# Input projections as seven products of mixed blocks, with values transposed, the residual in DRAM and fp32 scores

## The chip, the core and the metric

The kernel runs on one core of a Trainium2 chip. TensorE (PE in the profile, PEld its weight load) does the matmuls, VectorE (DVE), ScalarE (ACT) and GpSimd (POOL) the elementwise work, and SyncE's queue (SPq) issues every DMA. The metric is the device time of one execution in microseconds (us), lower is better.

## What is computed

One inference step of a two-layer decoder over 1024 prompt tokens and 8 sample tokens, model width 1024, all in fp32. Layer 0 is sliding-window attention (window 128, 32 heads of 64, 4 key/value heads), layer 1 is retention (4 heads, 256 wide in q and k, 512 in v). Each layer has one wide input projection, a gated mixer and an output projection:

```python
h = _rmsnorm(x, norm_g[i])
q, k, v, g = split(h @ w_in)                 # 1024 -> 4608 (layer 0) or 6144 (layer 1) features
logits = q k^T / 8 + bias(rel);  w = softmax with a learned sink;  o = w v      # layer 0
o = (q k^T * decay) v + q R * cross;  R = gamma R + k_dec^T v;  o = norm(o)     # layer 1
x = x + (silu(g) * o) @ w_out
y = _rmsnorm(x, final_norm_g)
```

## The kernel before

Activations stand with features on the partitions. The tokens go in two halves: half A is tokens 0 to 511 with the 8 samples (520 columns), half B is tokens 512 to 1023. An fp32 operand of a large matmul is split into a rounded high part and the rest (`hi` and `lo`, type fp32r), and a product is three matmuls: hi\*hi, lo\*hi, hi\*lo (lines 359 to 361).

**The weight stream.** `Stream` holds a list of jobs and of weight tiles (128x512). `wload` (line 171) loads a tile by DMA into `wraw` (3 buffers), ACT casts it to `whi` (line 175), and DVE and POOL in turn make `wlo = wraw - whi` (line 179). `AHEAD = 2` keeps two further tiles on the way, and `whi` and `wlo` have four buffers each. `proj_job` makes 128 features of the input projection from two tiles, in chunks of 260 columns (half A) or 512 (half B); `tok_job` makes values with tokens on the partitions; `out_job` and `out1_job` do the output projections, one tile for 128 features, and add to the residual `xa`, which stays in SBUF for one half at a time.

**The order of the work.** PE's order is written by hand: `spread` lays the jobs of the stream between the steps of the mixers. Layer 0 goes through 64 blocks of 4 heads and 128 queries (`att_scores`, `att_turn`, `att_values`), four key/value heads u for half A, then four for half B. Layer 1 goes through n = 0 to 7 (four heads for A, four for B). Each n has three stages: **a**, the output projection of n-1 (8 tiles); **b**, the gates of n+1 (two feature pairs); **c**, q, k and v of n+1 (four feature pairs of work). The other engines take their instructions in an order that the tile framework's scheduler writes at build time, and each works through its queue in order. `norm` makes the 8 normalised `hh`/`hl` tiles of a half, `rot_jobs` applies the rotary angles to q and k of layer 1, and `norm_stats` makes the row factors.

Of the kernel before, what the change touches and what calls it, by code (L numbers as in the profile page):

```python
# [19 lines left out]
P = 128  # L20
D = 1024
KT = 8
# [26 lines left out]

AHEAD = 2  # L50
SLACK = 600.0
# [7 lines left out]

class Stream:  # L60
# [4 lines left out]
    def __init__(self, load, ahead):  # L65
        self.load, self.ahead = load, ahead
        self.jobs = []
        self.todo, self.ready = [], []

    def push(self, srcs, fn, ns):  # L70
        self.todo += srcs
        self.jobs.append([fn, None, ns])
# [5 lines left out]
    def fetch(self, n):  # L78
        while self.todo and len(self.ready) < n:
            self.ready.append(self.load(self.todo.pop(0)))  # L80
# [30 lines left out]
def hybrid_step(ctx: ExitStack, tc: tile.TileContext, I: dict, O: dict):  # L111
# [4 lines left out]
    xp = ctx.enter_context(tc.tile_pool(name="xp", bufs=1))  # L116
# [16 lines left out]

    def chunks(T):
        return [(0, 512)] if T == HALF else [(0, 260), (260, 520)]


    xT = [None] * KT
    xdram = [[dp.tile([P, HALF], F32, name=f"xdram{hf}_{kt}") for kt in range(KT)] for hf in range(2)]
    xsmp = cp.tile([P, KT, NB], F32, name="xsmp")  # L140

    def load_x(srcs, T):
        for kt in range(KT):
            xa = xp.tile([P, HALF + NB], F32, name="xa", tag=f"x{kt}")
            sp.dma_start(xa[:, :T], srcs[kt])
            xT[kt] = xa

    def store_x(hf):
        for kt in range(KT):
            sp.dma_start(xdram[hf][kt], xT[kt][:, 0:HALF])  # L150
# [19 lines left out]

    def wload(src):
        raw = wp.tile([P, 512], F32, name="wraw", tag="wr", bufs=3)
        last[0] = sp.dma_start(raw, src)
        hi = wp.tile([P, 512], F32R, name="whi", tag="wh", bufs=4)
        act.copy(hi, raw)  # L175
        lo = wp.tile([P, 512], F32R, name="wlo", tag="wl", bufs=4)
        wctr[0] += 1
        eng = pool if wctr[0] % 2 else vec
        eng.tensor_tensor(out=lo, in0=raw, in1=r32(hi), op=ALU.subtract)  # L179
        return hi, lo  # L180

    stream = Stream(wload, 0)


    H = [None]

    def stats_rows(s, T):
# [5 lines left out]
        for b in range(4):  # L193
            pe.matmul(ps[:, b : b + 1], s[:, b * P : (b + 1) * P], ones[:, 0:1], start=True, stop=True)
        if T > HALF:
            pe.matmul(ps[:NB, 4:5], s[:, SMP], ones[:, 0:1], start=True, stop=True)
# [5 lines left out]
    def stats_spread(rs, T, tag):  # L202

        dg = ap_.tile([P, T], F32, name="dg", tag="sq", bufs=3)
# [7 lines left out]
        rb_ = ap_.tile([P, T], F32, name="rbc", tag=tag, bufs=1)  # L212
# [7 lines left out]
    def norm_stats(T, tag, out, stored=None):  # L220

        s = None
        for kt in range(KT):
            b = ap_.tile([P, T], F32, name="sqb", tag="sq", bufs=3)
            if stored is None:
                x = xT[kt][:, :T]
            else:
                x = b
                sp.dma_start(b, stored[kt])
            act.activation(b, x, AF.Square)  # L230
# [5 lines left out]
        rs = stats_rows(s, T)  # L236
        yield
        out.append(stats_spread(rs, T, tag))
        yield

    def norm(layer, T, rb_, src):

        hh, hl = [], []
        H[0] = (hh, hl, None, T)
        rb_ = [rb_.pop()]
        for kt in range(KT):
            f = ap_.tile([P, T], F32, name="hf", tag="sq", bufs=3)
            vec.scalar_tensor_tensor(out=f, in0=src(kt, f), scalar=gcol[:, layer, kt : kt + 1], in1=rb_[0], op0=ALU.mult, op1=ALU.mult)
            a = hp.tile([P, T], F32R, name=f"hh{kt}")
            b = hp.tile([P, T], F32R, name=f"hl{kt}")  # L250
            act.copy(a, f)
            (pool if kt % 2 else vec).tensor_tensor(out=b, in0=f, in1=r32(a), op=ALU.subtract)
            hh.append(a)
            hl.append(b)
            if kt % 2 and kt < KT - 1:
                yield
        if T > HALF:
            hs = cp.tile([P, KT, 40], F32R, name="hs", tag="hs")
            pool.memset(r32(hs), 0.0)
            for kt in range(KT):  # L260
                vec.tensor_copy(hs[:, kt, 0:NB], r32(hh[kt][:, SMP]))
                vec.tensor_copy(hs[:, kt, 32 : 32 + NB], r32(hl[kt][:, SMP]))
            H[0] = (hh, hl, hs, T)
        yield

    def stored_x(tiles, smp=False):
        def get(kt, f):
            sp.dma_start(f[:, 0:HALF], tiles[kt])
            if smp:
                vec.tensor_copy(f[:, SMP], xsmp[:, kt, :])  # L270
            return f

        return get

    def final_norm(hf, T):

        out = []
        yield from norm_stats(T, "rbc", out)
        for kt in range(KT):
            f = ap_.tile([P, T], F32, name="hf", tag="sq", bufs=3)  # L280
            vec.scalar_tensor_tensor(out=f, in0=xT[kt][:, :T], scalar=gcol[:, 2, kt : kt + 1], in1=out[0], op0=ALU.mult, op1=ALU.mult)
            sp.dma_start(O["yT"][kt, :, hf * HALF : hf * HALF + T], f)
        yield

    def final_part(c0, c1):

        w = c1 - c0
        xs = [xT[kt][:, c0:c1] for kt in range(KT)]
# [20 lines left out]
        if smp:  # L309
            fo = [ap_.tile([P, 2, w], F32, name="fo", tag="y", bufs=6) for _ in range(4)]  # L310
# [37 lines left out]
    def proj_job(src, evac):  # L348

        def run():  # L350
            hh, hl, _, T = H[0]
            out = [(gtile()[:, : c1 - c0], c0, c1) for c0, c1 in chunks(T)]
            for z in range(2):
                hi, lo = stream.tile()
                for ps, c0, c1 in out:
                    for i in range(4):
                        k = 4 * z + i
                        a, b = hi[:, i * P : (i + 1) * P], lo[:, i * P : (i + 1) * P]
                        pe.matmul(ps, a, hh[k][:, c0:c1], start=(k == 0), stop=False)  # L359
                        pe.matmul(ps, a, hl[k][:, c0:c1], start=False, stop=False)  # L360
                        pe.matmul(ps, b, hh[k][:, c0:c1], start=False, stop=(k == KT - 1))  # L361
                    if z:
                        evac(ps, c0, c1)
                    yield 12 * mm_ns(c1 - c0)

        stream.push([src[0], src[1]], run, 5200.0)

    def tok_job(srcs, width, smp, evac):


        per = 512 // width

        def run():
            hh, hl, hs, T = H[0]
            pss = [gtile()[:, :width] for _ in range(4)]
            if smp:
                pss.append(sps.tile([P, 1024], F32, name="vsp", tag="S")[:40, :width])
            for z in range(KT // per):
                hi, lo = stream.tile()
                for b, ps in enumerate(pss):  # L380
                    for i in range(per):
                        k = z * per + i
                        wh, wl = hi[:, i * width : (i + 1) * width], lo[:, i * width : (i + 1) * width]
                        if b < 4:
                            cs = slice(b * P, (b + 1) * P)
                            pe.matmul(ps, hh[k][:, cs], wh, start=(k == 0), stop=False)  # L386
                            pe.matmul(ps, hh[k][:, cs], wl, start=False, stop=False)  # L387
                            pe.matmul(ps, hl[k][:, cs], wh, start=False, stop=(k == KT - 1))  # L388
                        else:
                            pe.matmul(ps, hs[:, k, :], wh, start=(k == 0), stop=False)  # L390
                            pe.matmul(ps, hs[:, k, :], wl, start=False, stop=(k == KT - 1))
                    if k == KT - 1:
                        evac(b, ps)
                yield 14 * per * mm_ns(width)

        stream.push(list(srcs), run, KT * 14 * mm_ns(width))

    def sample_rows(ps, width):
        t = ap_.tile([NB, width], F32, name="srow", tag="s", bufs=SB)
        act.copy(t, ps[32 : 32 + NB, :])  # L400
        vec.tensor_tensor(out=t, in0=t, in1=ps[0:NB, :], op=ALU.add)
        return t

    def out_job(T, src, ys, fts):

        for ft in fts:
            def run(ft=ft):
                hi, lo = stream.tile()
                for c0, c1 in chunks(T):
                    ps = gtile()[:, : c1 - c0]  # L410
                    for k in range(4):
                        yh, yl = ys[k // 2]
# [4 lines left out]
                    x = xT[ft][:, c0:c1]  # L417
# [3 lines left out]
            stream.push([src[ft]], run, 2600.0)  # L421
# [3 lines left out]
    def new_y(tag="y", bufs=6):  # L425
# [931 lines left out]
```

## Time and profile before

| what | value |
|---|---|
| median of 3 runs | 1739.86 us (the fastest 1739.23) |
| profiled execution | 1736.38 us, span 1734.6 us |
| PE | 1697.7 us busy, 98% of the span |
| DVE, ACT, POOL | 1045.5 (60%), 841.1 (48%), 713.2 (41%) |
| granted TensorE clock | 0.994 |
| DMA | 211.31 MB, 122 GB/s over the span |

The span is the profiled execution from the first to the last instruction; the median stands 3.5 us above that execution's own time. A busy PE counts a matmul from its start to its modelled end, and matmuls overlap, so the spacing of starts is the cost of one, not its mean duration.

### The profile page before, as it was taken

How to read it: one execution, taken by the hardware profiler on the slowest of the kernel's cores; microseconds unless marked ns; L12 is line 12 of the kernel's file. 1: busy time of each engine (PE TensorE's matmuls, PEld its weight loads, DVE VectorE, ACT ScalarE, POOL GpSimd, SP SyncE). 2: the span in 40 equal slices, each digit the busy share in tenths (PEclk: the TensorE clock that was granted, in tenths of full speed). 3: DMA queues.
4: the chain of work that ended last, by engine and by line, in shares of the span. 5: the costliest groups of instructions: out<-in, count | busy, mean ns of one | idle time of the engine just before them, and what ended most of it. 6: DMA issues, size and time to landing. Idle time of an engine off the chain costs nothing.

```text
span 1734.6 us, 29003 instructions
## 1 busy us (share of the span) xinstructions
PE 1697.7 (98%) x10550; PEld 1450.0 (84%) x10550; DVE 1045.5 (60%) x2142; ACT 841.1 (48%) x1960; POOL 713.2 (41%) x670
## 2 busy tenths in 40 slices
PE   9999999999999999999999999999999999999997
PEld 8989999988887777779788797897777889888887
DVE  6777676784576565773475545566555655445366
ACT  5566465555556464654344444344343433433344
POOL 3244344353344343444334235344353353433534
PEclk9999999999999999999999999999999999999998
DMA  5523333333253323223476445466463262322323
GB/s 153 142 62 91 123 105 104 89 108 91 85 172 90 85 75 92 80 86 106 120 244 192 143 152 188 128 195 206 129 217 111 85 194 73 98 86 81 102 69 121
DMA packets 124174, 211.31 MB, mean 122 GB/s; under 512 B 17128, under 2 KB 28000, under 8 KB 124032
## 3 DMA queue, kind: packets, MB, share of 16 engines
q1 hardware_dynamic: 124032, 209.47, 39.5%
q8 instruction: 83, 1.36, 0.3%
q14 instruction: 59, 0.48, 0.1%
HBM read 177.57 MB, written 33.91 MB: 122 GB/s over the span
## 4 chain that ended last, share of the span: by engine, by line
PE 81%; DVE 5%; DMA 3%; ACT 2%; POOL 2%; issue 1%; SPq 0%; POOLq 0%; ACTq 0%; DVEq 0%
PE gemm L359 12%; PE gemm L360 12%; PE gemm L361 12%; PE gemm L386 4%; PE gemm L387 3%; PE gemm L388 3%; PE o L663 3%; PE gemm L1063 3%; PE gemm L1062 3%; PE gemm L1064 3%; PE gemm L414 3%; PE gemm L416 3%; PE gemm L415 3%; PE S L624 3%; PE pt L641 1%
## 5 line engine op out<-in xcount | busy, mean ns | idle before, releaser
L179 POOL TENSOR_TENSOR wlo<-wraw,whi 128x512 fp32r<-128x512 f32 x236 | 311.7, 1321 | 555.6 <-ACT whi L175 524.0
L359 PE MATMUL gemm<-hh,whi 128*128 128x260 f32 (+1 forms) x1584 | 520.9, 329 | 0.0
L361 PE MATMUL gemm<-hh,wlo 128*128 128x260 f32 (+1 forms) x1584 | 506.2, 320 | 0.4 <-POOL wlo L179 0.4
L360 PE MATMUL gemm<-hl,whi 128*128 128x260 f32 (+1 forms) x1584 | 506.2, 320 | 0.0
L175 ACT CAST whi<-wraw 128x512 fp32r<-128x512 f32 x472 | 290.5, 617 | 442.9 <-PE gemm L360 136.5
L359 PEld LDWEIGHTS gemm<-hh,whi 128*128 128x128 f32 x1584 | 298.2, 188 | 45.0 <-issue 15.3
L361 PEld LDWEIGHTS gemm<-hh,wlo 128*128 128x128 f32 x1584 | 298.0, 188 | 23.3 <-POOL wlo L179 0.6
L360 PEld LDWEIGHTS gemm<-hl,whi 128*128 128x128 f32 x1584 | 298.5, 188 | 20.2 <-issue 0.5
L179 DVE TENSOR_TENSOR wlo<-wraw,whi 128x512 fp32r<-128x512 f32 x236 | 190.1, 806 | 161.6 <-ACT whi L175 159.5
L431 POOL TENSOR_TENSOR yl<-yf,yh 128x256 fp32r<-128x256 f32 x128 | 107.3, 847 | 96.7 <-ACT yh L430 96.3
L414 PE MATMUL gemm<-yh,whi 128*128 128x260 f32 (+1 forms) x384 | 126.9, 330 | 4.4 <-DVE xa L418 4.4
L386 PE MATMUL gemm<-whi,hh 128*128 128x512 f32 (+1 forms) x320 | 123.1, 385 | 2.9 <-DVE ra L748 2.8
L598 ACT ACTIVATE L<-L,nm 128x128 f32<-128x128 f32 x256 | 99.8, 391 | 52.2 <-DVE nm L593 51.8
L1062 PE MATMUL gemm<-yh,whi 128*128 128x260 f32 (+3 forms) x384 | 124.7, 325 | 0.0
L416 PE MATMUL gemm<-yh,wlo 128*128 128x260 f32 (+1 forms) x384 | 123.2, 321 | 0.0
L415 PE MATMUL gemm<-yl,whi 128*128 128x260 f32 (+1 forms) x384 | 123.0, 320 | 0.0
L1063 PE MATMUL gemm<-yl,whi 128*128 128x260 f32 (+3 forms) x384 | 122.8, 320 | 0.0
L1064 PE MATMUL gemm<-yh,wlo 128*128 128x260 f32 (+3 forms) x384 | 122.8, 320 | 0.0
L388 PE MATMUL gemm<-whi,hl 128*128 128x512 f32 (+1 forms) x320 | 120.0, 375 | 2.0 <-DVE hl L1099 1.8
L387 PE MATMUL gemm<-wlo,hh 128*128 128x512 f32 (+1 forms) x320 | 120.4, 376 | 0.0
L602 POOL TENSOR_TENSOR L<-L,rsum 128x512 f32<-128x512 f32 x64 | 76.4, 1193 | 79.3 <-DVE rsum L601 45.4
L414 PEld LDWEIGHTS gemm<-yh,whi 128*128 128x128 f32 x384 | 72.6, 189 | 15.2 <-ACT whi L175 4.8
(246 smaller groups left out, 3141.8 us busy)
## 6 DMA issues: line engine op xcount, KB each, us to landing
wraw<-in_w_in SPq DMA_DIRECT2D x264, 256.0 KB
wraw<-in_w_out SPq DMA_DIRECT2D x136, 256.0 KB
wraw<-in_w_v SPq DMA_DIRECT2D x72, 256.0 KB
Rsm<-in_state SPq DMA_DIRECT2D x64, 256.0 KB
out_ret_state_sample<-Rsm SPq DMA_DIRECT2D x64, 256.0 KB
vrow<-vdram SPq DMA_DIRECT2D x32, 256.0 KB
bias<-bdram SPq DMA_DIRECT2D x16, 256.0 KB
xdram<-xa SPq DMA_DIRECT2D x16, 256.0 KB
```

The costliest lines, as they stand in the source:

```text
L175: act.copy(hi, raw)
L179: eng.tensor_tensor(out=lo, in0=raw, in1=r32(hi), op=ALU.subtract)
L359: pe.matmul(ps, a, hh[k][:, c0:c1], start=(k == 0), stop=False)
L360: pe.matmul(ps, a, hl[k][:, c0:c1], start=False, stop=False)
L361: pe.matmul(ps, b, hh[k][:, c0:c1], start=False, stop=(k == KT - 1))
L386: pe.matmul(ps, hh[k][:, cs], wh, start=(k == 0), stop=False)
L414: pe.matmul(ps, a, yh[:, k % 2, c0:c1], start=(k == 0), stop=False)
L415: pe.matmul(ps, a, yl[:, k % 2, c0:c1], start=False, stop=False)
L416: pe.matmul(ps, b, yh[:, k % 2, c0:c1], start=False, stop=(k == 3))
L1062: pe.matmul(ps, a, yh[:, k % 2, c0:c1], start=(k == 0), stop=False)
L1063: pe.matmul(ps, a, yl[:, k % 2, c0:c1], start=False, stop=False)
L1064: pe.matmul(ps, b, yh[:, k % 2, c0:c1], start=False, stop=(k == 3))
```

## The change

**Projections.** A pair of 128-feature blocks, over the two quarters of a half's tokens (256 columns and 256 or 264) and the two halves of the 1024 input features, is a 2x2 product of blocks. It is now made by seven products of mixed blocks instead of eight (`unit_job`). The seven activation mixtures of a half are made once by `mixtures`, each split into hi and lo; the seven weight mixtures are made for each pair by `mixed`, from four loaded tiles, each split into hi and lo. A product is 12 matmuls and takes one split tile. Raw weight tiles have 7 buffers, and loads go 3 further tiles ahead (`DEEP`).

```diff
+    def mixed(wa, wb):
...
+        def third():
+            minus(d["a"], d["b"], d["a"], vec)
+            d["t"] = wtile()
+            return wsplit(minus(d["t"], d["d"], d["a"], vec), vec)
+        return [
+            Weights(get(a=wa[0]), lambda: wsplit(d["a"], pool)),
+            Weights(get(c=wa[1]), lambda: wsplit(d["c"], pool)),
+            Weights(get(b=wb[0], d=wb[1]), third),
+            Weights(None, lambda: wsplit(d["a"], pool)),
+            Weights(None, lambda: wsplit(minus(d["b"], d["d"], d["b"], pool), vec)),
+            Weights(None, lambda: wsplit(d["d"], pool)),
+            Weights(None, lambda: wsplit(minus(d["c"], d["c"], d["t"], pool), vec)),
+        ]
+    def mixtures(k, f1, f2, T):
...
+        part(0, k, a1, pool)
+        part(1, k, b1, vec)
+        part(6, k, b2, vec)
+        vec.tensor_tensor(out=b2, in0=a2, in1=b2, op=ALU.add)
+        pool.tensor_tensor(out=a2, in0=a1, in1=a2, op=ALU.subtract)
+        vec.tensor_tensor(out=a1, in0=b2, in1=a1, op=ALU.subtract)
+        part(2, k, a1, vec)
+        part(3, k, b2, pool)
+        part(4, k, a2, vec)
+        vec.tensor_tensor(out=b1, in0=b1, in1=a1[:, 0:QT], op=ALU.subtract)
+        part(5, k, b1, pool)
+    def unit_job(T, wa, wb, dst, done):
...
+                for k in range(4):
+                    hh, hl = [x[:, :n] for x in hc[c][k]]
+                    wh, wl = hi[:, k * P : (k + 1) * P], lo[:, k * P : (k + 1) * P]
+                    pe.matmul(ps[:, :n], wh, hh, start=(first and k == 0), stop=False, skip_group_check=not first)
+                    pe.matmul(ps[:, :n], wh, hl, start=False, stop=False, skip_group_check=not first)
+                    pe.matmul(ps[:, :n], wl, hh, start=False, stop=(k == 3), skip_group_check=not first)
...
+        stream.push(mixed(wa, wb), run, 84 * mm_ns(QT))
```

**Evacuation.** The seven products leave through three accumulators; ACT copies three quarters out of PSUM, DVE adds to three of them, and the last one goes straight on. In `rot_jobs` two of the four quarters of a pair are then read from SBUF, not from PSUM.

**Values** come out with features on the partitions like the rest and are turned by PE transposes (`turn` in layer 0, `ret_turn_v` in layer 1); the sample rows are transposes too.

**Scores.** The two matmuls for each head (fp32r, hi and lo of one head stacked to 128 rows) become one fp32 matmul of 64 rows for each head, two heads on the two halves of the rows, and the factor 0.125 moves into the addition of the bias.

```diff
-        for e in range(4):
-            for n, kk in enumerate((kh, kl)):
-                pe.matmul(S[:, e, w0:256], q[e][:, cs], kk[:, b * P + w0 : b * P + 256], start=(n == 0), stop=(n == 1))
+        for j in range(2):
+            for par in range(2):
+                r = slice(64 * par, 64 * par + 64)
+                pe.matmul(S[:, 2 * par + j, w0:256], q[j][r, cs], kk[r, b * P + w0 : b * P + 256], start=True, stop=True)
```

**The residual** is read from DRAM and written back for every output tile, through two buffers `xa`; the last two heads keep it in SBUF.

```diff
+                xa = get(ft)
                 hi, lo = stream.tile()
...
+                put(ft, xa)
```

In the built program POOL gets 404 instead of 236 of the `wlo` subtractions and 168 subtractions of raw tiles, DVE 320 instead of 236 and 168; ACT casts 724 tiles instead of 472.

How the rows stand now, first on POOL in stage c of a head of half B. Before, from the gates' last `yl` (stage b) to the values' tiles (`rf` and `rl` are the rotary parts of q and k, `wlo` the split of a weight tile):

```order
L179 TENSOR_TENSOR wlo<-wraw,whi 128x512 x2
L431 TENSOR_TENSOR yl<-yf,yh 128x2x128 x2
L179 TENSOR_TENSOR wlo<-wraw,whi 128x512
L749 TENSOR_TENSOR rf<-rf,ra 128x512 x2
L753 TENSOR_TENSOR rl<-rf,rh 128x512
L179 TENSOR_TENSOR wlo<-wraw,whi 128x512
L753 TENSOR_TENSOR rl<-rf,rh 128x512
L179 TENSOR_TENSOR wlo<-wraw,whi 128x512
L749 TENSOR_TENSOR rf<-rf,ra 128x512 x2
L179 TENSOR_TENSOR wlo<-wraw,whi 128x512 x4
```

Now, the same place up to the second rotary pair (`wraw<-wraw` is a mixture of raw tiles, `cq` a quarter out of PSUM):

```order
L518 TENSOR_TENSOR yl<-yf,yh 128x2x128 x2
L185 TENSOR_TENSOR wlo<-wraw,whi 128x512 x2
L213 TENSOR_TENSOR wraw<-wraw 128x512 x2
L862 TENSOR_TENSOR cq<-cq,cos 128x256 x2
L185 TENSOR_TENSOR wlo<-wraw,whi 128x512
L864 TENSOR_TENSOR rf<-rf,cq 128x256 x2
L185 TENSOR_TENSOR wlo<-wraw,whi 128x512
L868 TENSOR_TENSOR rl<-rf,rh 128x256 x2
L185 TENSOR_TENSOR wlo<-wraw,whi 128x512 x2
L213 TENSOR_TENSOR wraw<-wraw 128x512
L862 TENSOR_TENSOR cq<-cq,cos 128x256 x2
```

Where a feature pair had two `wlo` on POOL, it has four and two mixtures of raw tiles, beside the rotary work.

Second, on PE, a block's scores `S` in layer 0. Before:

```order
L361 MATMUL gemm<-hh_334,wlo 128x260
L624 MATMUL S<-khh,qe 128x256
L624 MATMUL S<-kll,qe 128x256
L624 MATMUL S<-khh,qo 128x256
L624 MATMUL S<-kll,qo 128x256
...
L688 MATMUL ss<-kT,qbd 16x128 x4
```

Now, with the projection's matmuls of 264 columns ahead of it:

```order
L433 MATMUL gemm<-h_1h,whi 128x264
L434 MATMUL gemm<-h_1l,whi 128x264
L435 MATMUL gemm<-h_1h,wlo 128x264
L735 MATMUL S<-kk,qf 128x256 x4
L799 MATMUL ss<-kT,qbd 16x128 x4
```

Eight score matmuls of a block (the four rows of before stand there twice) have become four.

More of the change, by code (lines that the diff above doesn't have):

```diff
@@ L132, in hybrid_step @@
     TA, TB = HALF + NB, HALF
[L134 to L150, printed above, removed]
+    QT = 256
+    QS = QT + NB
+    xdram = [[dp.tile([P, HALF + NB], F32, name=f"xdram{hf}_{kt}") for kt in range(KT)] for hf in range(2)]
     cst = cp.tile([P, C_END], F32, name="cst")
@@ L266, in stored_x, with part @@
[L266 to L273, printed above, removed]
+    HC = {}
+    def part(c, k, src, eng):
+        if k % 2 == 0:
+            HC[c, k // 2] = [hp.tile([P, 2, QS], F32R, name=f"h{c}_{k // 2}{n}", tag=f"h{c}_{k // 2}{n}") for n in "hl"]
+        w = src.shape[-1]
+        hh, hl = [t[:, k % 2, :w] for t in HC[c, k // 2]]
+        act.copy(hh, src)
+        eng.tensor_tensor(out=hl, in0=src, in1=r32(hh), op=ALU.subtract)
+        H[0][c][k] = (hh, hl)
@@ new lines, in new_h, with load_pieces, norm @@
+    def new_h(T):
+        H[0] = [[None] * 4 for _ in range(7)] + [T]
+    def load_pieces(f, src, T):
+        sp.dma_start(f[:, 0:QT], src[:, 0:QT])
+        sp.dma_start(f[:, QS : QS + T - QT], src[:, QT:T])
+    def norm(layer, T, rb_, stored):
+        new_h(T)
+        rb_ = [rb_.pop()]
+        for k in range(4):
+            fs = []
+            for kt in (k, k + 4):
+                f = ap_.tile([P, 2 * QS], F32, name="hf", tag="hf", bufs=3)
+                load_pieces(f, stored[kt], T)
+                if T > HALF and kt < 4:
+                    pool.memset(f[:, QT:QS], 0.0)
+                for c0, c1, o in ((0, QT, 0), (QT, T, QS)):
+                    x = f[:, o : o + c1 - c0]
+                    vec.scalar_tensor_tensor(out=x, in0=x, scalar=gcol[:, layer, kt : kt + 1], in1=rb_[0][:, c0:c1], op0=ALU.mult, op1=ALU.mult)
+                fs.append(f)
+            mixtures(k, fs[0], fs[1], T)
+            yield
@@ L309, in final_part @@
         if smp:
[L310 removed]
+            fo = [ap_.tile([P, 2, w], F32, name="fo", tag="g", bufs=4) for _ in range(4)]
             fs = [fo[kt // 2][:, kt % 2, :] for kt in range(KT)]
@@ L346, in mm_ns, with product @@
         return 0.4168 * n + 2
-    def proj_job(src, evac):
+    def unit_job(T, wa, wb, dst, done):
         def run():
-            hh, hl, _, T = H[0]
-            out = [(gtile()[:, : c1 - c0], c0, c1) for c0, c1 in chunks(T)]
-            for z in range(2):
+            hc = H[0]
+            assert T == hc[7]
+            w = T - QT
+            def product(ps, c, n, first):
                 hi, lo = stream.tile()
[L355 to L404, printed above, removed]
+                for k in range(4):
+                    hh, hl = [x[:, :n] for x in hc[c][k]]
[3 more added lines that the diff above has]
+                    pe.matmul(ps[:, :n], wl, hh, start=False, stop=(k == 3), skip_group_check=not first)
@@ new lines, in dst, with done @@
+        def dst(j, q):
+            if not d["q"]:
+                d["q"] += [ap_.tile([P, 2 * QS], F32, name="qf", tag="q", bufs=8)[:, :T] for _ in range(2)]
+                if not hf:
+                    d["qs"] = sm.tile([P, 2, NB], F32, name="qs", tag="qs", bufs=4)
+            return d["q"][j][:, span(q, T)]
+        def done(j, q, ps):
+            t = d["q"][j][:, span(q, T)]
+            if not hf:
+                vec.tensor_tensor(out=t, in0=ps, in1=RB[0][:, span(q, T)], op=ALU.mult)
+                if q:
+                    act.copy(d["qs"][:, j, :], d["q"][j][:, SMP])
+            elif j == 0 and q == 1:
+                act.copy(t, ps)
@@ new lines, in done @@
+        def done(j, q, ps):
+            g = d["g"]
+            t = g[:, j, span(q, T)]
+            if not hf:
+                (vec if j == 0 and q == 1 else pool).tensor_tensor(out=t, in0=ps, in1=RB[0][:, span(q, T)], op=ALU.mult)
+            elif j == 0 and q == 1:
+                act.copy(t, ps)
+            if j == 0 and q == 1:
+                act.activation(g[:, :, :T], g[:, :, :T], AF.Silu)
+                if not hf:
+                    d["gs"] = sm.tile([P, 2, NB], F32, name="gs", tag="gs", bufs=4)
+                    vec.tensor_copy(d["gs"], g[:, :, SMP])
@@ new lines, in first_pair @@
+    def first_pair(k):
+        for kt in (k, k + 4):
+            x, g = xs[kt], gcol[:, 0, kt : kt + 1]
+            q = ap_.tile([P, 2, HALF + NB], F32, name="sq0", tag="g", bufs=4) if k % 2 == 0 else sq[kt - 1]
+            sq[kt] = q
+            for c0, c1, o in ((0, QT, 0), (QT, TA, QS)):
+                act.activation(q[:, k % 2, c0:c1], x[:, o : o + c1 - c0], AF.Square)
+                vec.tensor_scalar(out=x[:, o : o + c1 - c0], in0=x[:, o : o + c1 - c0], scalar1=g, scalar2=None, op0=ALU.mult)
+        mixtures(k, xs[k], xs[k + 4], TA)
```

643 lines of the change are left out of this document (345 added, 298 removed).

## The prediction

> **What bounds the kernel now.** I read the page's busy times first, then the slices, then the chain that ended last.
>
> ```profile
> PE 1697.7 (98%) x10550; PEld 1450.0 (84%) x10550; DVE 1045.5 (60%) x2142; ACT 841.1 (48%) x1960; POOL 713.2 (41%) x670
> PE   9999999999999999999999999999999999999997
> PE 81%; DVE 5%; DMA 3%; ACT 2%; POOL 2%; issue 1%; SPq 0%; POOLq 0%; ACTq 0%; DVEq 0%
> ```
>
> PE is busy in every slice, holds 81% of the chain, and no other engine is over 60%. So a matmul less is time less, as long as the others can feed PE faster. Whether they can is read from single stages. A window is cut where ACT casts the first weight tile of a stage:
>
> ```profile
> 122.10:216.00 93.90, 92.11 (x775) 86.14 (x774) 66.45 (x159) 50.56 (x149) 38.25 (x38) 1.00 0.35 104
> 365.00:398.30 33.30, 31.30 (x222) 28.00 (x223) 22.99 (x51) 17.30 (x51) 17.45 (x15) 1.00 0.36 103
> 1026.70:1082.20 55.50, 54.69 (x376) 45.97 (x375) 27.82 (x52) 23.30 (x46) 25.28 (x26) 1.00 0.61 194
> 1460.70:1487.90 27.20, 27.20 (x161) 23.91 (x160) 13.78 (x34) 10.55 (x21) 11.35 (x12) 1.00 0.24 71
> 1487.90:1537.60 49.70, 49.70 (x223) 40.52 (x222) 18.64 (x31) 17.12 (x31) 23.41 (x20) 1.00 0.35 108
> ```
>
> The columns are length, then PE, PEld, DVE, ACT, POOL busy. The rows are four blocks' phases of one key/value head in layer 0 (half A), the phase in which half B's norm is made, stage c for half A, stage b and stage c for half B. PE is full in all of them; the others have half their time left.
>
> **What PE gains.** The cost of a matmul is the spacing of starts:
>
> ```profile
> 400.21 0.39 PE L360 MATMUL gemm<-hl,whi 128*128 128x512 f32 x1
> ...
> 403.91 0.40 PE L361 MATMUL gemm<-hh,wlo 128*128 128x512 f32 x1
> ...
> 1693.01 0.28 PE L1062 MATMUL gemm<-yh,whi 128*128 128x260 f32 x1
> ...
> 1694.21 0.29 PE L1063 MATMUL gemm<-yl,whi 128*128 128x260 f32 x1
> ...
> 1695.54 0.28 PE L1062 MATMUL gemm<-yh,whi 128*128 128x256 f32 x1
> ...
> 1696.97 0.28 PE L1062 MATMUL gemm<-yh,whi 128*128 128x256 f32 x1
> ```
>
> 16, 10 and 12 intervals: 0.231 us for 512 columns, 0.120 for 260, 0.119 for 256, and by the slope 0.122 for 264. A feature pair of half A was 2x8x3 products in two chunks, 96 x 0.120 = 11.5, and is 60 x 0.122 + 24 x 0.119 = 10.2; of half B 48 x 0.231 = 11.1, now 84 x 0.119 = 10.0. There are 33 such pairs in each half (17 in layer 0, 16 in layer 1): 33 x (1.3 + 1.1) = 79. The values were 112 matmuls of 256 in layer 0 (96 for half B): 13.3 and 11.4, now 10.2 and 10.0; in layer 1, for two pairs, 112 or 96 of 512: 25.9 and 22.2, now 20.4 and 20.0, four heads each. That is 4.5 + 30.8 = 35. Turning values back adds 144 transposes; at 0.11 apiece (a block's four `oT` stand inside 0.6 us in the trace) some 16, with the samples' 17.
>
> A block's scores go from eight matmuls to four fp32 ones of 64 rows. The nearest rows are the old scores, and `o`, fp32 with 256 columns too, two at a time on halves of the columns:
>
> ```profile
> 404.24 0.65 PE L663 MATMUL o<-ptc,vb 128*64 128x256 f32 x4
> 404.72 0.60 PE L663 MATMUL o<-ptp,vb 128*64 128x256 f32 x4
> 405.25 0.50 PE L359 MATMUL gemm<-hh,whi 128*128 128x512 f32 x1
> ...
> 408.14 0.28 PE L624 MATMUL S<-khh,qe 128*128 128x256 f32 x1
> ...
> 409.09 0.39 PE L359 MATMUL gemm<-hh,whi 128*128 128x512 f32 x1
> ```
>
> Two `o` side by side take 0.48 to 0.53 us, so four scores take 1.0 if the row halves run side by side too, and 2.0 if not; the old eight took 0.95. No row shows row halves. I take 1.0, from the nearest row: 64 x 0.05 = +3; the other end is +64. The Trainium skill's page "TensorEngine Tiling (Array Packing)", section Tiling Modes, says that tiles of the array, of rows as of columns, run in parallel, which gives the 3; no run here shows it for rows.
>
> PE: -79 - 35 + 17 + 3 = **-94**.
>
> **What the feed costs.** A product uses up a split tile in 12 x 0.12 = 1.44 us, where a tile lasted 2.8 to 2.9. The splits:
>
> ```profile
> L179 POOL TENSOR_TENSOR wlo<-wraw,whi x236: 1262/1291/2149, 4.7 to 1714.9; 128x512 fp32r<-128x512 f32 x118
> L179 DVE TENSOR_TENSOR wlo<-wraw,whi x236: 649/692/1781, 7.8 to 1716.9; 128x512 fp32r<-128x512 f32 x118
> L175 ACT CAST whi<-wraw 128x512 fp32r<-128x512 f32 x472 | 290.5, 617 | 442.9 <-PE gemm L360 136.5
> L749 POOL TENSOR_TENSOR rf<-rf,ra 128x512 f32<-128x512 f32 x16 | 23.5, 1492 | 12.1 <-DVE ra L748 12.0
> L753 POOL TENSOR_TENSOR rl<-rf,rh 128x260 fp32r<-128x260 f32 x16 | 11.4, 742 | 0.5 <-ACT rh L752 0.5
> ```
>
> Per pair POOL now has four splits and two mixtures, 6 x 1.29 = 7.7 us, DVE three and two, 5 x 0.69 = 3.5, ACT 7 x 0.62 = 4.3. Each is below PE's 10.0 alone. But POOL and DVE are not independent, and this decides the case. Why do the medians and maxima of one shape lie so far apart?
>
> ```profile
> 62.34 0.68 DVE L179 TENSOR_TENSOR wlo<-wraw,whi 128x512 fp32r<-128x512 f32 x1
> 62.61 1.56 POOL L179 TENSOR_TENSOR wlo<-wraw,whi 128x512 fp32r<-128x512 f32 x1 [1.19 <-ACT whi L175]
> ...
> 538.92 1.04 POOL L602 TENSOR_TENSOR L<-L,rsum 128x512 f32<-128x512 f32 x1
> 539.03 1.48 DVE L179 TENSOR_TENSOR wlo<-wraw,whi 128x512 fp32r<-128x512 f32 x1 [1.58 <-ACT whi L175]
> 539.92 1.10 POOL L648 TENSOR_SCALAR_AFFINE_SELECT ptp<-ptp 128x512 f32<-128x512 f32 x1
> 540.44 0.41 DVE L665 TENSOR_TENSOR yf<-o,g 128x256 f32<-128x256 f32 x1
> ```
>
> At 539.03 DVE starts a subtraction of two SBUF tiles while POOL works; it ends at 540.51, 0.55 after POOL's end at 539.96, and POOL's next ends 0.51 after that. At 62.61 it is POOL that ends late, 1.15 after DVE's end at 63.02. So such an operation on DVE and one on POOL exclude each other: 0.55 and 1.15 us of a common resource, only the first 0.14 of either lies under the other. `yf`, which reads PSUM, takes its 0.41 us. The Trainium skill's page "SBUF — State Buffer", section SBUF: two separate sides, has the pair held for a whole instruction; by that a stage below would cost the 0.14 for some 30 alternations, 4.4 us, more; the rows above show the overlap, so the sum goes without it.
>
> *Stage c, half B* (eight tiles to each of POOL and DVE before; 28 tiles now). POOL: 23.4 - 8 x 1.29 - (4 x 1.49 + 2 x 1.41, the rotary) + 24 x 1.29 + 10 x 0.74 = 43.2. DVE's operations on two SBUF tiles: 20 x 0.55, and 14 rotary ones of half the width, 3.9. Together 58.1 less 4.4 of overlap: 53.7. PE: 49.7 - 44.4 + 40.0 = 45.3. Over by 8.4. *Stage c, half A*: POOL 25.3 - 10.3 - 9.7 + 31.0 + 7.4 = 43.7, with DVE's 14.9 and some eight `Rsm` at 0.6, less 4.4, 59; PE 55.5 - 48.9 + 40.7 = 47.3. Over by 11.7. PE can have three tiles (4.3 us) in hand at the start, so at the least 4.1 and 7.4 remain; above, queues are in order and POOL is not always fed. There are four such stages of each half (the first as the kernel passes to layer 1): 46 at least, 80 without the tiles in hand. I take 60. Stages a and b have room for their 8 and 14 tiles (b: POOL 11.4 + 8 x 1.29 = 21.7, DVE's 5.5, against PE's 25).
>
> *The activation mixtures.* DVE's part of a half's norm grows from 8 x 0.86 + 4 x 0.72 = 9.8 to 4 x 11 operations at 0.43 = 19, POOL's from 6.7 to 12.
>
> ```profile
> L248 DVE SCALAR_TENSOR_TENSOR hf<-hf,gcol,rbc 128x512 f32<-128x512 f32 x16 | 13.7, 860 | 11.9 <-DMA hf<-xdram 11.0 <-DMA hf<-in_x 0.9
> L593 DVE TENSOR_TENSOR nm<-nm,nsink x64: 141/161/1225, 68.9 to 790.0; 128x4 f32<-128x4 f32 x64
> 6.25 0.56 PE L386 MATMUL gemm<-whi,hh 128*128 128x256 f32 x1
> ```
>
> In the window at 365 DVE then has 23.0 + 9 + 8 more tile operations, 5.5, so 37.5, and up to 12 more if 40 of its operations meet a POOL that holds half the time for 0.6: 37 to 50 against PE's 31. I take +13 there, the same for the norm ahead of layer 1's first gates (DVE holds 29 of 43.7 there now), +4 for the one under layer 1: **+30** (14 to 42). *The start*: PE began at 6.25 with the first two tiles of x; the first product now needs one mixture from all eight, behind three quarters of their 44 + 16 operations on DVE, some 14 us later: **+12** (5 to 18). *Layer 0, half A*: a head's phases (window at 122) hold DVE 66 of 94; about 50 operations on SBUF meet POOL, which goes from 38 to 61; the small ones (`nm`) show what that is, 0.16 alone and 1.2 behind POOL. 50 x 0.2 more of the time x 0.6 = 6 each: **+8** in all where PE has no slack left (0 to 30).
>
> *The residual* is loaded 2 tiles ahead and each load waits for a store.
>
> ```profile
> SPq L145 <- DMA xdram<-xa: 25.4, 13, 3.0
> ```
>
> A wait of 2.0 (25.4 / 13) and two issues of 0.35 make 2.7 to 3.7 us a tile on the queue, weight loads behind it; PE needs 24 x 0.12 = 2.9 and the mixers' share beside it, 3.4 to 4.1. Hidden, **+4** (0 to 60, if 128 tiles lose half a microsecond).
>
> **Sum.** 1734.6 - 94 + 60 + 30 + 12 + 8 + 4 = 1754.6 of span; with 1.8 around it and the 3.5 by which the median stands above that execution, **1760**.
>
> **Rivals.**
> (1) *PE stays the bound*: the tiles in hand and the slack of stages a and b carry stage c, the mixtures lie under attention. Then -94 and the start's and a few: 1734.6 - 94 + 25 + 5 = 1671. For it: 98% on PE and POOL at 41%. Against: POOL alone has 43 of 45 us in stage c.
> (2) *DVE's queue becomes the bound in attention, too* (slower). DVE is in order; when it waits for POOL, the softmax's small steps and the evacuations stand behind it. It decides once DVE's own 70 us and its waits pass PE's 85 in a head's phase: with POOL at 70% of it, 55 operations x 0.7 x 0.55 = 21, so 91, and PE's gain of 9 us a head is gone in 8 heads (+45 beyond the 8), stage c goes to 80 and the mixtures to 42: 1760 + 45 + 20 + 12 + 20 for late tiles = 1857.
> (3) *Scores one after the other*: +61, some of it where PE has slack: 1810.
> (4) *The residual's queue* holds weight loads back: +40, 1800.
> That the seven products are not made is excluded by the order shown above.
>
> **Chances.** The forecast 0.42 (its own range 1715 to 1810), (1) 0.26, (2) 0.18, (3) 0.07, (4) 0.07. 2% of 1739.86 is what a measurement of this kernel can tell: below 1705 faster, above 1775 slower. Faster 0.24 (nearly all of (1)); the same 0.35 (0.30 of the forecast, the rest of (1) and part of (4)); slower 0.41. To leave out no more than a tenth at each end the range goes from the middle of (1) to that of (2): 1665 to 1850.
>
> **What would show it.** PE below 96% with its idle time in stage c, ended by `wlo` of POOL or DVE; POOL over 1100 us; `wlo` on DVE with a mean well above 0.8; scores of a block in 1.0 us; PE's starts still 0.12 apart. A chain with over 75% PE and a span below 1700 proves (1); idle PE in layer 0 behind DVE proves (2).

## The result and the profile after

The changed kernel takes **2139.04 us** (median of four, 2136.17 to 2147.01) against 1739.55: a ratio of 1.2306, 95% interval 1.2263 to 1.235. The forecast of 1760 was 379 us too low and its range (to 1850) missed; slower had the largest chance of the three, 0.41, and was right in sign alone. One of the four runs of the kernel before was a slow one, 3581.42 us, and the ratio leaves it out.

From the page of the changed kernel, the busy times, PE's slices and the granted clock:

```profile
PE 1780.7 (83%) x12046; PEld 1570.6 (74%) x12046; DVE 1529.9 (72%) x2640; ACT 1028.1 (48%) x2471; POOL 1272.7 (60%) x1093
PE   6888989887988998968887888787888778888887
PEclk5999999998999999979999899898899889999998
```

PE went from 98% to 83%, and no other engine is over 72%: nobody is the bound all the time. New is the last row, the granted clock in tenths. A mean clock of 0.909 over 2135.2 us is 389 us at half rate; it was 0.994, 21 us. PE's busy time rose to 1780.7 us although there are fewer columns to stream.

Where the time went is read by stretches with the same work in both: from the first scores to half B's first, to layer 1, to its half B, and to the end. Before, then after (length, then PE, PEld, DVE, ACT, POOL busy, granted clock, DMA share, GB/s):

```profile
65.00:437.00 372.00, 361.49 (x2915) 331.98 (x2914) 261.09 (x598) 215.13 (x614) 157.13 (x152) 1.00 0.34 97
437.00:852.00 415.00, 412.53 (x2343) 334.08 (x2342) 247.78 (x498) 225.72 (x580) 173.78 (x173) 1.00 0.32 96
852.00:1316.00 464.00, 456.99 (x2648) 377.14 (x2646) 269.41 (x502) 202.05 (x387) 192.40 (x174) 1.00 0.56 180
1316.00:1727.00 411.00, 404.98 (x2209) 348.14 (x2207) 222.49 (x447) 162.04 (x306) 167.17 (x147) 1.00 0.32 98
```

```profile
106.00:548.00 442.00, 377.55 (x2870) 331.44 (x2866) 342.45 (x658) 233.81 (x678) 286.61 (x261) 0.93 0.36 107
548.00:1020.00 472.00, 416.44 (x2838) 351.08 (x2839) 331.90 (x583) 261.02 (x687) 302.24 (x267) 0.94 0.39 116
1020.00:1617.00 597.00, 478.06 (x2905) 412.93 (x2905) 439.83 (x680) 269.24 (x551) 334.70 (x276) 0.89 0.51 163
1617.00:2127.00 510.00, 429.95 (x2978) 403.70 (x2977) 340.12 (x589) 215.20 (x442) 292.74 (x237) 0.93 0.36 111
```

Layer 0 lost 70 and 57, layer 1 133 and 99, and 41 went before the first scores. What PE waited for, the longest sums (us in all, times, longest):

```profile
PE vtp L974 <- DVE ktl L1001: 70.4, 20, 7.5
PE pt L752 <- POOL L L710: 36.1, 15, 8.8
PE gemm L435 <- DVE wlo L185: 30.5, 19, 2.5
PE gemm L433 <- ACT g L453: 29.4, 16, 4.8
PE vtp L974 <- DVE gr L941: 26.8, 4, 7.6
```

In layer 0 the largest is `pt`, the transpose of the softmax weights, which waits for POOL's last step on them (`L`), and behind it the copies of the projections' accumulators (`g`, `qf`); PE's waits there come to 120 us, against 13 before.

One place stands out that the forecast doesn't have: `vtp`, the turn of layer 1's values, with 97 us in 24 waits. One of them, in the order of time on PE, and then what DVE does meanwhile:

```profile
1202.14 0.38 PE L991 MATMUL skt<-cst,rf 128*128 128x128 f32 x2
1210.11 1.09 PE L974 MATMUL vtp<-cst,vf 128*128 128x128 f32 x4 [7.58 <-DVE gr L941]
...
1211.42 0.63 PE L490 MATMUL gemm<-yl,whi 128*128 128x512 f32 x1
1211.85 0.63 PE L491 MATMUL gemm<-yh,wlo 128*128 128x512 f32 x1
```

```profile
1204.78 0.69 DVE L931 BATCH_NORM_STATS2 bst<-ro 128x6 f32<-128x512 f32 x1
1205.39 1.36 DVE L961 TENSOR_TENSOR Rl<-R,Rh 128x512 fp32r<-128x512 f32 x1
1206.67 1.75 DVE L213 TENSOR_TENSOR wraw<-wraw 128x512 f32<-128x512 f32 x1
1208.34 0.34 DVE L993 SCALAR_TENSOR_TENSOR scf<-skt,cst 128x128 f32<-128x128 f32 x1
```

`vtp` takes a buffer of the small PSUM pool (`wps`, two tiles). One holds `skt`, the scores issued just ahead of it; the other holds `ro` until ACT has made the group norm's output `on` from it. All 24 waits end 0.15 us after DVE's `ktl`, its last read of `skt` (here it ends at 1209.96), and in all 24 `on` was not yet finished: it is the buffer of `skt` that `vtp` gets. DVE's queue has a split of the state and a weight mixture, slowed by POOL, ahead of that read. Eleven of the waits are only 2.5 to 2.6 us long, the time that the reads of `skt` take when little stands ahead of them. PE is in order: the output projection behind `vtp` starts as soon as `vtp` has. When it does, its starts are 0.43 us apart (1211.42, 1211.85), not 0.23: the clock has halved. Over all matmul starts, what lies above the full-clock spacing in half-clock stretches sums to an estimated 123 us (115 to 145 by how waits inside a stretch are counted; 5 before); idle PE is the larger part, 354 us of the span against 37 before.

The feed, by groups:

```profile
L185 POOL TENSOR_TENSOR wlo<-wraw,whi 128x512 fp32r<-128x512 f32 x404 | 568.3, 1410 | 382.4 <-ACT whi L183 354.6
...
L185 DVE TENSOR_TENSOR wlo<-wraw,whi 128x512 fp32r<-128x512 f32 x320 | 313.1, 980 | 108.1 <-ACT whi L183 104.6
...
L213 POOL TENSOR_TENSOR wraw<-wraw 128x512 f32<-128x512 f32 x168 | 245.8, 1467 | 88.9 <-DVE wraw L213 55.6
...
L213 DVE TENSOR_TENSOR wraw<-wraw 128x512 f32<-128x512 f32 x168 | 184.3, 1097 | 20.0 <-POOL wlo L185 17.0
```

A split takes 0.69 us on DVE without POOL beside it; the means here are 0.98 and 1.10. The forecast's exclusion stands in this trace, too: 185 of DVE's splits and mixtures began while POOL had a two-input operation of 128x512 running with over 0.25 us to go, and every one of them ended 0.54 to 0.55 us after POOL's. What DVE's operations take above the shortest of their kind sums to some 426 us (155 before).

### The profile page after: what moved, and what is told of

Its sections match the earlier page's. It is cut to its first block, busy times and chain, and to the rows that moved or that the text cites. A ratio compares the mean times of both kernels' runs of the same rounds, so it can differ in the third digit from the quotient of the medians.

```text
span 2135.2 us, 34638 instructions
## 1 busy us (share of the span) xinstructions
PE 1780.7 (83%) x12046; PEld 1570.6 (74%) x12046; DVE 1529.9 (72%) x2640; ACT 1028.1 (48%) x2471; POOL 1272.7 (60%) x1093
## 5 line engine op out<-in xcount | busy, mean ns | idle before, releaser
L185 POOL TENSOR_TENSOR wlo<-wraw,whi 128x512 fp32r<-128x512 f32 x404 | 568.3, 1410 | 382.4 <-ACT whi L183 354.6
L433 PE MATMUL gemm<-h_0h,whi 128*128 128x256 f32 (+1 forms) x1176 | 381.9, 325 | 125.8 <-ACT g L453 29.4
L435 PE MATMUL gemm<-h_0h,wlo 128*128 128x256 f32 (+1 forms) x1176 | 354.2, 301 | 33.8 <-DVE wlo L185 30.5
L433 PE MATMUL gemm<-h_1h,whi 128*128 128x256 f32 (+1 forms) x1176 | 349.1, 297 | 16.9 <-ACT h_1h L296 16.9
L434 PE MATMUL gemm<-h_1l,whi 128*128 128x256 f32 (+1 forms) x1176 | 348.8, 297 | 7.5 <-DVE h_1l L297 5.5
L434 PE MATMUL gemm<-h_0l,whi 128*128 128x256 f32 (+1 forms) x1176 | 350.4, 298 | 1.3 <-POOL h_0l L297 1.3
L435 PE MATMUL gemm<-h_1h,wlo 128*128 128x256 f32 (+1 forms) x1176 | 348.0, 296 | 0.0
L213 POOL TENSOR_TENSOR wraw<-wraw 128x512 f32<-128x512 f32 x168 | 245.8, 1467 | 88.9 <-DVE wraw L213 55.6
L435 PEld LDWEIGHTS gemm<-h_0h,wlo 128*128 128x128 f32 x1176 | 241.6, 205 | 38.9 <-DVE wlo L185 34.7
L434 PEld LDWEIGHTS gemm<-h_0l,whi 128*128 128x128 f32 x1176 | 241.7, 206 | 2.8 <-POOL h_0l L297 1.8
```

Source lines behind the costliest of these rows:

```text
L213: eng.tensor_tensor(out=out, in0=x, in1=y, op=ALU.subtract)
L433: pe.matmul(ps[:, :n], wh, hh, start=(first and k == 0), stop=False, skip_group_check=not first)
L434: pe.matmul(ps[:, :n], wh, hl, start=False, stop=False, skip_group_check=not first)
L435: pe.matmul(ps[:, :n], wl, hh, start=False, stop=(k == 3), skip_group_check=not first)
```

## The experiments

All are measured against the kernel before (1737 to 1740 us); "changed" is the kernel after, 2139.

**Three parts of the change, and the seven products as a whole.** The turn later in PE's order:

```diff
-        if b:
-            ret_turn_v(n, b)          # at the end of ret_scores
+        def tv(b, f):                 # one stage later in spread's list
+            return lambda: (ret_turn_v(n, b), f())
```

> Values of layer 1 are turned one or two products after the scores instead of right behind them. Theory A (the change put waits of PE's own into its order: 24 places skt then vtp that hold 102 us of idle PE, 20 that follow on an accumulator being copied): the 102 us go, and of the half-clock time that follows idle stretches (123 us lost beside 340 us more idle time, a third of an us for each) another 30: 2139 - 130 = 2010. Theory B (DVE and POOL are late everywhere since they exclude each other on two-SBUF operations; PE then waits at the next place): 2090 to 2139.

2101.17: 38 us less, inside theory B's range. Its trace still holds 66 of the 97 us of waits at `vtp`, each ended by `ktl` as before. So the place was only a part of it; whether the two buffers are the rest is tried below.

An accumulator for each product:

```diff
-            t = product(a, 2, w, False)
+            a = gtile()
+            t = product(a, 2, w, True)    # and so for products 4, 5 and 6
```

> Every product gets an accumulator of its own (four in turn) and adds onto nothing, which leaves the sums of products out; instructions, sizes and copies stay. PE's waits for the copies of an accumulator (88 us on ACT, 22 on DVE) have three products' time instead of one. Theory A: 110 us and a third of that in half-clock time go: 1990 to 2010. Theory B: 2090 to 2139.

2107.78, 31 us less, again inside theory B's range. PE's idle time ahead of the first matmul of a product fell from 126 to 37 us, but that ahead of its first `wlo` matmul rose from 34 to 80: the feed took the place.

The weight mixtures left out:

```diff
-            eng.tensor_tensor(out=out, in0=x, in1=y, op=ALU.subtract)
-            return out
+            return x
```

> The weight mixtures are left out (the raw tile is split in their place): POOL and DVE lose 168 subtractions of two SBUF tiles each, 246 and 184 us of busy time, nothing else changes. Theory B (the feed by DVE and POOL): 2139 - 200 = 1940 or less. Theory A: PE's own waits stay, 2070 to 2130.

1954.68, **184 us** less, close to theory B's 1940. 336 subtractions cost that much (leaving them out also frees the raw tile that one of them wrote to). The waits of `pt` for POOL in layer 0 fall from 36 to 8 us and layer 0's loss from 127 to 38; the waits at `vtp` stay, 88 us.

Eight plain products, each weight tile split once, for both quarters `q`:

```diff
-            t = product(a, 0, w, True)
...
+            for f in range(2):
+                ps[f, 0], ps[f, 1] = gtile(), gtile()
+                for z in range(2):
+                    hi, lo = stream.tile()
+                    for q in range(2):        # 12 matmuls into ps[f, q]
```

> Eight plain products of the same quarters in place of seven mixed ones: 96 matmuls and four weight splits a pair, no mixtures of weights or activations, four accumulators, no sums in place; the transposed values, the residual in DRAM and the fp32 scores stay. If the loss is the seven products' alone: 1700 to 1760. If the turned values carry 102 us of waits and 30 of half clock with them in any form: 1840. If the residual or the scores cost more than they seem to: above 1900.

1909.07, the third case's range. So 170 of the 400 us come without the seven products, and `vtp` holds 86 us of waits here too, with DVE at 53%. PE's own order makes that wait, not only a busy DVE.

**What else there is, and one part alone.** The turn through the matmul pool, at the later place of the first run:

```diff
-        vt = wps.tile([P, 4, P], F32, name="vtp", tag="w")
+        vt = gtile().rearrange("p (a b) -> p a b", a=4)
```

> The eight plain products of before, and the values of layer 1 turned through an accumulator of the matmul pool (four buffers) one or two products after the scores, in place of the small pool of two right behind them. Theory A (PE's own order and that pool make the wait): its 91 us and some 30 of half clock in layer 1 go, 1909 - 120 = 1790. Theory B (DVE and ACT are late, so PE waits at the next place): above 1860.

1819.07: 90 us, theory A, though 30 less than expected. Of the 170 us, 80 are left; a run below gives 18 of them to the residual, 22 go before the first scores, and no run parts the rest.

The turn so, with an accumulator for each product and no weight mixtures (the three edits above together, in the changed kernel):

> Seven products, with three things taken out together: the weight mixtures (raw tiles are split in their place), the sums in place (an accumulator for each product), and the turn of the values moved as in the run with eight products. If the three losses add: 2139 - 185 - 31 - 120 = 1800. If each hid another one: PE's work of 1560 with the start's 40 and the rest of its waits, 1690 to 1730, below the eight products.

1827.53, 28 us above the first case, which had 120 for the turn: the three add (311 us together; 184, 31 and, below, 86 alone make 302).

All weight work on DVE:

```diff
-            return wsplit(d["w"], pool if wctr[0] % 2 else vec)
+            return wsplit(d["w"], vec)
...
-            Weights(get(a=wa[0]), lambda: wsplit(d["a"], pool)),
+            Weights(get(a=wa[0]), lambda: wsplit(d["a"], vec)),
```

> All 724 splits and all 336 mixtures of weight tiles are made by DVE, none by POOL; the arithmetic is the same. If the mutual exclusion of DVE and POOL is what costs: the weights hold the common resource for 1060 x 0.69 = 731 us instead of 488 x 0.55 + 572 x 1.15 = 926, and DVE's 426 us of waiting mostly go: 1950 to 2050. If it is DVE's queue itself, with evacuations and softmax steps behind the weights: 2139 to 2250.

2029.11, **110 us less** by moving 572 operations from an engine with 60% to the one with 72%. Its page and its group:

```profile
PE 1731.5 (86%) x12046; PEld 1530.8 (76%) x12046; DVE 1599.4 (79%) x3212; ACT 1035.0 (51%) x2471; POOL 508.4 (25%) x521
...
L185 DVE TENSOR_TENSOR wlo<-wraw,whi 128x512 fp32r<-128x512 f32 x724 | 535.2, 748 | 99.6 <-ACT whi L183 93.4
```

DVE has 572 operations more and only 70 us more busy time: a split is back at 0.75, and 426 us above the shortest became some 208. That is as the exclusion has it. But the run doesn't part it from the other thing that the move does: a split that took 1.41 us on POOL takes 0.75 on DVE, so that a tile is ready sooner.

The change's diff of the scores, in the kernel before:

> The kernel before with one part of the change alone: fp32 scores of 64 rows, two heads on the row halves, 0.125 in the addition of the bias; q and k are kept in fp32 and not split. In the changed kernel a pair of scores takes 0.306 us, so a block 0.62 instead of 0.95 us: 64 x 0.33 = 21 us less, 1718, if PE bounds attention. If another engine sets the end there: 1735 to 1745.

1737.03, ratio 0.9995 (0.9984 to 1.0007): no change that the runs can tell. The expectation misread its rows. It took the 0.306 us between starts for a pair of scores; an fp32 matmul is two records, and a block (the first row here, four matmuls) lasts until the next matmul starts:

```profile
154.59 1.13 PE L619 MATMUL S<-kk,qf 64*128 64x256 f32 x8
155.66 0.39 PE L359 MATMUL gemm<-hh,whi 128*128 128x260 f32 x1
```

1.07 us, against 0.95 before: the forecast's 1.0, with the row halves side by side.

**The clock, the pure gain, the residual.** 30 matmuls (3.6 us) that nobody reads, ahead of each `vtp`:

```diff
+            fill = gtile()[:, 0:QT]
+            for _ in range(30):
+                pe.matmul(fill, d["qh"][0][:, 0:P], d["qh"][0][:, 0:QT], start=True, stop=True)
             ret_turn_v(n, b)
```

> The changed kernel with 30 matmuls of 256 columns (3.6 us) that nobody reads ahead of each of the 24 turns of values, where PE stands idle for 4.3 us on average. Theory A (idle stretches bring the half clock, and the half clock is a cost of its own): the fill takes the place of idle time, the granted clock of layer 1 rises, and what the removal of the same wait gave the eight products (38.7 to 14.9 us of half-clock loss) comes here too, 25 to 35 us: 2105 to 2115. Theory B (the half clock has another cause, or costs nothing where the others are late): 2139 to 2180.

2129.85: with 720 matmuls more, 9 us less, a difference that the intervals don't part from none (ratios 1.2211 to 1.2283 here, 1.2263 to 1.235 for the changed kernel). Layer 1's half A, filled:

```profile
1018.00:1608.00 590.00, 508.67 (x3269) 448.10 (x3268) 440.33 (x677) 268.02 (x547) 337.11 (x277) 0.92 0.52 164
```

597 became 590, 0.89 became 0.92. So a busier PE keeps more of the clock, but the time is not the 25 to 35 us of theory A. The run doesn't say what the clock alone is worth: the fill takes 3.6 us, and 14 of the 24 waits were shorter than 3 us, so that there it also holds PE up.

The activation mixtures left out, in the run with three things taken out:

```diff
-        part(2, k, a1, vec)
...
+        for c, o in ((2, 0), (4, 3), (5, 1)):
+            H[0][c][k] = H[0][o][k]
```

> As the run with three things taken out, and the activation mixtures too: four unmixed parts a tile pair are split, the other three products use them again. If the mixtures of the activations cost what the milestones show (28 us to the first scores, 19 in the norm of half B, 14 and more in the norms of layer 1): 1828 - 60 = 1770. If they hide under attention: 1815 to 1828.

1811.84, 16 us: near the second case. The first scores came at 80 instead of 94 us; the rest was hidden.

Twelve of a pair's matmuls left out, in the eight plain products with the turn moved:

```diff
-                        for k in range(4):
+                        for k in range(z, 4):
```

> The eight plain products with moved turns, 12 of a pair's 96 matmuls left out; four splits a pair, all else as there. If PE sets the time there, the gain the change was to bring shows itself: 84 units x 12 x 0.12 = 121, 1819 - 121 = 1698. If the others hold PE as soon as it is faster: above 1760.

1728.56: 91 of the 121 us. Fewer matmuls are time where the feed stays as it was.

A third buffer for the residual's tiles in the same form (the edit stands at two places):

```diff
-            xa = ap_.tile([P, HALF + NB], F32, name="xa", tag="xs", bufs=2)
+            xa = ap_.tile([P, HALF + NB], F32, name="xa", tag="xs", bufs=3)
```

> The eight plain products with moved turns, and a third buffer for the residual's tiles, so that a load is issued one tile earlier. DVE waits 76 us for residual tiles with two. If that is part of the 80 us by which this form stands above the kernel before: 1785 to 1805. If DVE's wait is hidden: 1815 to 1822.

1801.36, 18 us. DVE's waits for residual tiles from DRAM fell from 91 to 20 us: two buffers do hold it.

**One loss or two, and 83 us that remain.** The turn through the matmul pool at the later place, in the changed kernel, alone and then with all weight work on DVE:

> The changed kernel with one edit: values of layer 1 turned through an accumulator of the matmul pool, one or two products after the scores. With eight products the edit gave 90 us. If the wait is a loss of its own, beside the feed: 2139 - 90 - the half clock it leaves = 2030 to 2050. If the late feed takes its place: 2090 to 2110, as with the later place alone.

2052.57: 86 us, 3 us above the first case's range. The later place alone gave 38 of them, the other pool the rest; no wait at the turn of layer 1's values is left in the trace.

> That edit, and all weight splits and mixtures on DVE: two edits that leave the arithmetic as it is. If exclusion and turn add: 2139 - 110 - 90 = 1940. If one hides the other: 1990 to 2030.

1940.16, as expected: they add. With both edits, and all of the arithmetic, the change is still slower, by a ratio of 1.1159 (1.1096 to 1.1222). Of the 208 us by which its profiled execution is the longer, 104 are layer 0's, where `pt` still waits 45 us for POOL, 68 layer 1's, and 36 the start's.

Between the seven products without mixtures (1812) and the plain ones with as many matmuls (1729) lie 83 us. The tiles of a pair split four times, not seven:

```diff
-            Weights(None, lambda: wsplit(d["a"], pool)),
+            Weights(None, lambda: d["as"]),      # the split of the first use
```

> As the run without any mixtures, and the four tiles of a pair are split once each instead of seven times (six buffers for the parts): 84 matmuls and four splits a pair as in the run of plain products at 1729, but seven products of four accumulators with three additions by DVE. If the three further splits hold the rest of the loss: 1730 to 1750. If it is the additions and the seven separate products: 1795 to 1812.

1735.86, ratio 0.999 (0.9972 to 1.0009): 76 us for three further splits a pair (ACT, and DVE or POOL), and seven products without sums in place stand 7 us above the plain ones (1729). The run also has six buffers for the split tiles, not four; that share wasn't tried apart.

Read upward the runs make a chain: 1736 (seven products, no mixtures, four splits, turn moved), +76 for seven splits, +16 for activation mixtures, +311 for weight mixtures, sums in place and the turn's wait: 2139. No run with the whole arithmetic beat the kernel before.

## Why the prediction was wrong, step by step

- **PE's gain (-94).** Sound as far as it was tried: starts stand 0.12 us apart as forecast, a block's scores take 1.07 us, and in the plain products 121 us of matmuls left out gave 91. In the changed kernel none of it shows as time.
- **The turned values (+16) are the first step that failed.** The sum priced the transposes by their duration and never placed them in PE's queue. The step named no buffer; the order shows `vtp` straight behind `skt`, in a pool of two. That cost 86 us, more than the forecast had for stage c.
- **Stage c (+60): right in kind, too small.** Cut at matmul starts, the stage takes 64 to 65 us in half A (forecast 59) and 62, 61, 57 and 56 in half B (forecast 53.7; its POOL sum adds up to 42.7, not 43.2). Above the 47.3 and 45.3 us forecast for PE that is 107 us in these seven, where the sum had 60 for eight. In the last two, split tiles end 6 to 7 us of PE's 9 to 10 us of waits; in half A what empties the accumulators (ACT's copies, DVE's additions) ends more of them than the splits do, and all seven stages have 10 to 17 us at half clock. The Trainium skill's page "SBUF — State Buffer", section SBUF: two separate sides, has the port pair that the two share held for a whole instruction, by which 4.4 us were to be added to half B's 53.7. These lengths, with such other waits in them, don't decide it; the 185 operations above, which end 0.55 us after POOL's where one takes 0.69 alone, bear out the 0.14 of overlap that the sum took. The windows of one head's stages a, b and c of half B, cut at matmul starts; before they took 31.1, 27.2 and 49.7, cut at casts:

```profile
1776.60:1817.70 41.10, 34.99 (x251) 33.02 (x250) 20.76 (x47) 12.16 (x22) 13.82 (x11) 0.96 0.38 117
1817.70:1851.10 33.40, 30.12 (x226) 28.36 (x225) 22.11 (x44) 19.30 (x40) 21.41 (x19) 1.00 0.43 136
1851.10:1907.00 55.90, 46.18 (x345) 44.74 (x344) 43.65 (x56) 23.91 (x52) 47.42 (x38) 0.91 0.27 82
```

  "Stages a and b have room" is what fell: 10 and 6 us lost, with POOL at 14 and 21 of the stretch. It is no engine's sum that fills them: `vtp` stands in both, and its waits are 6.1 us of this stage a and 2.5 of this b.
- **The feed is the step that failed by most.** Weight mixtures cost 184 us and the further splits 76, where the sum had 60 for stage c and 8 elsewhere. Layer 0's loss of 127 us, most of which goes with the mixtures, had those 8 and a part of the +30. The sums asked in each stage whether an engine has time; PE's queue asks whether this tile is ready now, after a subtraction, ACT's cast and another subtraction on three in-order queues. That this chain is the way from 44 us of work to a late tile is argued from the waits (POOL 354.6 us for `whi`), not shown.
- **Sums in place** weren't priced: 31 us.
- **The start (+12)** became 41. Part of it isn't in the projections at all: the squares of x's eight tiles are now summed by PE itself, in 80 matmul records instead of 10. They take 14 us, all of them at half clock although the profile has PE busy throughout:

```profile
L247 PE MATMUL nps<-ones,sq x80: 163/352/352, 37.4 to 51.4; 128*128 128x1 f32 x64, 128*8 128x1 f32 x16
```

- **Activation mixtures (+30)**: 16 in the one run that takes them out. **The residual (+4)**: 18 in the form with eight products.
- **The half clock** wasn't in the sum at all, though a forecast with 60 us of idle PE should have asked for it. The Trainium skill's page "TensorE: Matmul & The Clock Gate", section Part 1: The HAM clock gate, says that the clock halves after an idle window of about 3.4 us, counted in windows that run free. The trace agrees on the windows: all but one of the 64 half-clock stretches last a multiple of 3.41 us, and all begin on one grid of that step. It differs on idle: in the 3.41 us ahead of a stretch PE was busy for up to 53%, for more than 5% in 55 of the 64, and every full-clock window of the grid with PE busy under 47% was followed by half clock (a matmul's end is modelled). Half of the stretches had no idle gap of 3 us in or next to that window, so shorter waits are enough. The page takes the ramp for under 1% of a span; here it took some 123 us, 6%, since it came back 64 times.
- **The rivals.** (2), DVE's queue in attention too, was the nearest in kind and 282 us short; in the trace PE waits there for POOL's `L` and ACT's copies. Most signs listed under what would show the forecast right came true (PE below 96%, POOL over 1100, `wlo` on DVE above 0.8, starts 0.12 us apart) and fitted a result 379 us away: they had no upper bound. One did not: PE's idle time isn't mainly in stage c behind `wlo`, which ended 34 of its 354 us.

## What to carry to other kernels

A new instruction on an in-order engine has a place as well as a duration: ask which buffer it takes, who frees that, and what stands behind it. Where the engine that sets the time is made faster by work for the others, ask for the latency from tile to tile and not only for the busy share, and count the operations that exclude each other as one engine. And stalls on TensorE can be paid for again in half clock: here some 123 us beside 354 of idle time, and stalls shorter than 3 us were enough for it.

## What was not expected of the hardware

Moving 572 operations off a POOL that was idle 40% of the time onto the busier DVE made the kernel 110 us faster. 720 matmuls that nobody reads, put where PE stood idle, didn't make it slower, and the granted clock rose from 0.909 to 0.923. And the clock halved after windows of 3.41 us in which PE had still been busy for up to half of the time.
